# Down-projection by seven products: another order, and three of four weight sums by accumulating DMA

## The chip, the cores and the metric

The kernel runs on one core of one Trainium2 chip. The metric is the device time in microseconds of one execution; lower is better. Engines are named as in the profile: PE is TensorE's matmul, PEld its weight load, DVE is VectorE, ACT is ScalarE, POOL is GpSimd, SP is the queue that issues most DMAs.

## The reference, cut to what matters

One layer of a hybrid decoder on 256 positions of 2048 channels, all in float32. The change touches only the last product of the feed-forward part:

```
h = rmsnorm(x, g_ffn)                                   # 256 x 2048
u = causal_dwconv(h @ w_up, ffn_conv_w) + ffn_conv_b    # 256 x 11264
gate, val = split(u, 2)                                 # 256 x 5632 each
x = x + (silu(gate) * val) @ w_down                     # w_down: 5632 x 2048
out = rmsnorm(x, g_final)
```

## The kernel before

A float32 product is made of three matmuls: each operand is split into a coarse part `hi` and a rest `lo`, and hi x hi, hi x lo and lo x hi are added up in PSUM. A weight tile is therefore loaded as raw float32 by a DMA, ScalarE copies it to `hi` (rounding), VectorE subtracts `hi` from the raw tile into `lo`, and TensorE streams both. There are three buffers each for `raw`, `hi` and `lo`, so a split can be at most three tiles ahead of TensorE.

The feed-forward part works in six groups of hidden channels: five of 1024 and one of 512. `up` computes the hidden channels of a group from 8 tiles of `w_up` per 512 channels (24 matmuls a tile). The down-projection of a group follows one group later, and its products are put between the up tiles by hand: `sched` takes three up tiles, then an up tile and a product in turn, and after the last up tile of the group two products in a row. In the last, smaller group the products are packed more tightly.

The down-projection of a group of 1024 hidden channels and 1024 output channels (`p` is 0 or 1, so two of these per group) is one "block": a 2 x 2 block product done with seven products instead of eight. The stationary operands are the sums of activation blocks that `make_forms` makes once per group (`turn`, `sums`). The moving operands are weight blocks and sums of them, each 128 x 2048 float32 (1 MiB): products 0 to 6 use b11, b11+b12, b11+b12+b22, b12+b22, b22, b21 and b11+b12+b22+b21. These are held in three buffers of the tile `ffn` (`rawd`; a fourth part of `ffn` is `u_raw`). A sum is made in place, once the product that needed the earlier state of the buffer has been split. Two ways are used: `add`, a VectorE tensor_tensor of two buffers (L247), and `add_far`, a DMA issued by GpSimd that reads the second operand from DRAM and adds it into the buffer (L244). Plain loads are issued by SP (L241).

In class `Blocks` the products are done in the order 0, 1, 2, 3, 4, 5, 6. After the split of product 0, b12 is added to b11 by VectorE and b22 to b12 by DMA; after that of product 1, b22 is added to b11 by VectorE; after that of product 3, b21 is loaded into b12's buffer and added to b11 by DMA. After the splits of products 4, 5 and 6 the next block's b11, b22 and b12 are loaded into the buffers that have come free. The same class serves the output projection (`OutBlocks`) and part of the first up-projection (`UpBlocks`). Nine blocks of the down-projection are of class `Blocks`; the tenth is `Plain`, four ordinary products. The instructions between the head and the last group are ordered per engine by the framework's scheduler, which works from the program's order and its own estimate of when operands are ready; the order is fixed when the kernel is built.

Of the kernel before, what the change touches and what calls it, by code (L numbers as in the profile page):

```python
# [9 lines left out]
F32 = mybir.dt.float32  # L10
F32R = mybir.dt.float32r
AF = mybir.ActivationFunctionType
ALU = mybir.AluOpType
AX = mybir.AxisListType

P = 128
# [8 lines left out]
def kernel(  # L25
# [6 lines left out]
    nc = tc.nc  # L32
# [9 lines left out]
    x, mem, out = x[0], mem[0], out[0]  # L42
# [4 lines left out]
    wpool = ctx.enter_context(tc.tile_pool(name="wpool", bufs=3))  # L47
# [37 lines left out]
    def columns_turn(st, n, at):  # L85
        pt = bank(f"pcol_{at}")
        with tc.high_priority():
            nc.tensor.transpose(pt[:, :n], st[:n, :], ident[:n, :n])
            nc.vector.tensor_copy(cols[:, at : at + n], pt[:, :n])
        return at + n  # L90
# [13 lines left out]
    loaded, split = {}, {}  # L104
# [100 lines left out]
    group_of = []  # L205
# [7 lines left out]
    N_PROD = 7  # L213

    class Blocks:
# [12 lines left out]
        def at(self, name):  # L228
            return (self.seq + {"b11": 0, "b22": 1, "b12": 2, "b21": 2}[name]) % 3

        def buf(self, name):
            return rawd[self.at(name)]
# [16 lines left out]
        def split(self, i, idx):  # L249
            raw = self.buf(("b11", "b11", "b11", "b12", "b22", "b21", "b11")[idx])  # L250
            hi, lo = split[i] = [
                wpool.tile([P, 4, 512], F32R, tag=t, name=f"{t}_{i}") for t in ("hi", "lo")
            ]
            nc.scalar.activation(hi, raw, AF.Copy)  # L254
            nc.vector.tensor_tensor(lo, raw, hi.bitcast(F32), op=ALU.subtract)  # L255
            if idx == 0:
                self.add("b11", "b12")
                self.add_far("b12", "b22")
            elif idx == 1:
                self.add("b11", "b22")  # L260
            elif idx == 3:
                self.load("b21")
                self.add_far("b11", "b21")
            elif self.next is not None and idx >= 4:
                names = Plain.ORDER if isinstance(self.next, Plain) else ("b11", "b22", "b12")
                self.next.load(names[idx - 4])

    class Plain(Blocks):

# [1 line left out]
        ORDER = ("b11", "b21", "b12", "b22")  # L271

        def buf(self, name):
            return rawd[(self.seq + self.ORDER.index(name)) % 3]

        def split(self, i, idx):
            raw = self.buf(self.ORDER[idx])
# [38 lines left out]
    for gi in range(len(group_of) - 1):  # L316
        for p in range(2):

            kind = Plain if gi == len(group_of) - 2 and p == 1 else Blocks
            blocks.append(kind(len(blocks), gi, p))  # L320
            if len(blocks) > 1:
                blocks[-2].next = blocks[-1]
# [32 lines left out]
    prods = []  # L355
    for gi, (a, n) in enumerate(group_of):
        n_t = 8 * n
        if not prods:
            after = [0] * n_t
        elif n == 2:  # L360
            after = [0, 0, 0] + [1] * 12 + [2]
        else:
            after = [0, 0, 0, 1, 1, 1, 2, 6]
        assert sum(after) == len(prods)
        for t in range(n_t):
            if gi == 0:
                if t == 0:
                    for o in UP_ORDER:
                        sched.append(("up", 0, o) if isinstance(o, int) else ("mixed", UpBlocks.U, o[1]))
                continue  # L370
            sched.append(("up", a + t // 8, t % 8))
            for _ in range(after[t]):
                sched.append(prods.pop(0))
        if gi < len(group_of) - 1:
            prods = []
            for b in blocks[2 * gi : 2 * gi + 2]:
                n = len(b.ORDER) if isinstance(b, Plain) else N_PROD
                prods += [("plain" if isinstance(b, Plain) else "prod", b, i) for i in range(n)]
    for what, a, b in sched:
        if what == "up":  # L380
            w, q = part_of(a, b)
# [7 lines left out]
    a0, n = group_of[-1]  # L389
# [145 lines left out]
    at = columns_turn(*stage_g)  # L535
# [13 lines left out]
    for k in range(KC):  # L549
        i, j = divmod(k, 4)  # L550
# [41 lines left out]
    at = columns_turn(*stage_x)  # L592
# [20 lines left out]
    for i in range(KC // 4):  # L613
        ti = KC // 4 + i
        advance(ti + 1 + LOAD_AHEAD, 0)
        hi, lo = split.pop(ti)
# [201 lines left out]
    for j in range(0, NCONV, 2):  # L818
# [4 lines left out]
        for mi in range(2):  # L823
            t = spool.tile([P, S], F32, tag="w1k", name=f"cc_{j + mi}", bufs=6)
# [9 lines left out]
        for mi in range(2):  # L834
# [4 lines left out]
            t = spool.tile([P, S], F32, tag="w1k", name=f"cv_{j + mi}", bufs=6)  # L839
# [12 lines left out]
        for mi in range(2):  # L852
            t = spool.tile([P, S], F32, tag="w1k", name=f"cb_{j + mi}", bufs=6)
# [108 lines left out]
    rawd = [ffn[:, 1 + i, :].rearrange("p (j c) -> p j c", c=512) for i in range(3)]  # L962
# [306 lines left out]
```

## Time and profile before

| | |
|---|---|
| runs, median of 3 | 1039.08 us (1039.08 to 1039.49) |
| profiled execution, its own time | 1039.66 us |
| profiled execution, span | 1037.9 us |
| granted TensorE clock | 0.997 |
| HBM read | 222.06 MB, 216 GB/s over the span |

The span is the time from the first to the last instruction that the profile shows; the execution's own time is a little longer. A stretch of a profile gives the busy time of each engine in microseconds, with the number of its instructions in brackets, then the granted clock, the mean busy share of the sixteen DMA engines and GB/s. A timeline row gives start, duration, engine, line, operation, the tiles written and read, and in square brackets the engine's idle time just before and what ended it. In the chain of work that ended last, a row gives start, duration, engine, tile, line and the number of instructions.

### The profile page before, as it was taken

The page shows a single profiled execution, that of the slowest core. Times are in us where ns is not written, and L with a number is a line of the kernel's source. Part 1 is how long each engine was busy: PE and PEld are TensorE (multiplying, and loading weights), DVE is VectorE, ACT ScalarE, POOL GpSimd, SP SyncE. Part 2 cuts the span into 40 slices and gives each one's busy share as a digit, 9 for nine tenths or more (in the row PEclk, how much of TensorE's full clock was granted, in tenths as well). Part 3 has the DMA queues.
Part 4 walks back from the last instruction along what each step waited for, and adds up shares of the span by engine and source line. Part 5 has one row for each costly group of instructions (what it writes and reads, how often), then busy time and mean ns, then how long its engine had stood idle before and what let it go on. Part 6 is the DMA issues. An engine that isn't in the chain of part 4 may idle for free.

```text
span 1037.9 us, 12624 instructions
## 1 busy us (share of the span) xinstructions
PE 1026.7 (99%) x4970; PEld 861.9 (83%) x4970; DVE 820.5 (79%) x866; ACT 601.8 (58%) x654; POOL 64.1 (6%) x97
## 2 busy tenths in 40 slices
PE   9999999999999999999999999999999999999996
PEld 7888888888888888888888888888888888888885
DVE  5677686777869688978779787797878978789776
ACT  5965454544556576655556556665566655665653
POOL 0023500000001000000000000000000000000000
PEclk9999999999999999999999999999999999999998
DMA  9765465557775687687966878668786697867832
GB/s 321 254 214 191 146 201 175 191 191 240 220 262 176 155 259 243 197 253 203 259 224 201 255 204 260 219 199 258 208 260 216 194 265 209 258 218 191 282 118 81
DMA packets 125157, 224.97 MB, mean 217 GB/s; under 512 B 3970, under 2 KB 36010, under 8 KB 124970
## 3 DMA queue, kind: packets, MB, share of 16 engines
q1 hardware_dynamic: 113450, 201.09, 57.2%
q0 software_dynamic: 11616, 23.07, 13.6%
q8 instruction: 39, 0.64, 0.2%
q14 instruction: 20, 0.16, 0.1%
q10 hardware_dynamic: 32, 0.01, 0.0%
HBM read 222.06 MB, written 2.10 MB: 216 GB/s over the span
## 4 chain that ended last, share of the span: by engine, by line
PE 98%; DMA 1%; DVE 0%; SPq 0%; DVEq 0%; issue 0%; ACT 0%
PE pu L981 42%; PE pp_a L921 9%; PE pp_b L921 5%; PE pp_c L921 2%; PE pa_cb L468 2%; PE pa_pv L468 2%; PE pa_cx L468 2%; PE pa_cc L468 2%; PE po L504 2%; PE pp L1127 2%; PE po L501 2%; PE po L507 2%; PE pz L1079 2%; PE pm_a L1024 2%; PE pa_q L468 1%; PE pk L558 1%
## 5 line engine op out<-in xcount | busy, mean ns | idle before, releaser
L981 PE MATMUL pu<-hi,h2T 128*128 128x512 f32 x1280 | 409.4, 391 | 0.0
L132 DVE TENSOR_TENSOR lo<-raw,hi 128x2048 fp32r<-128x2048 f32 (+3 forms) x148 | 314.7, 2128 | 70.9 <-ACT hi L131 69.9
L131 ACT ACTIVATE hi<-raw 128x2048 fp32r<-128x2048 f32 (+3 forms) x148 | 264.3, 1789 | 110.5 <-issue 34.7
L981 PEld LDWEIGHTS pu<-hi,h2T 128*128 128x128 f32 x1280 | 240.3, 188 | 49.4
L981 PE MATMUL pu<-lo,h2T 128*128 128x512 f32 x640 | 249.5, 390 | 0.0
L255 DVE TENSOR_TENSOR lo<-ffn,hi 128x2048 fp32r<-128x2048 f32 x70 | 160.3, 2290 | 72.0 <-ACT hi L254 72.0
L254 ACT ACTIVATE hi<-ffn 128x2048 fp32r<-128x2048 f32 x70 | 134.0, 1916 | 105.1 <-PE pu L981 75.0
L981 PEld LDWEIGHTS pu<-lo,h2T 128*128 128x128 f32 x640 | 120.2, 188 | 25.1 <-DVE lo L132 0.7
L921 PE MATMUL pp_a<-hi,sums 128*128 128x512 f32 x288 | 94.5, 389 | 0.0
L1089 DVE SCALAR_TENSOR_TENSOR t<-pz,cols,t 128x255 f32<-128x255 f32 (+1 forms) x176 | 79.6, 478 | 10.2 <-ACT t L1087 9.2
L1087 ACT ACTIVATE t<-pz,cols 128x256 f32<-128x256 f32 x88 | 46.9, 558 | 48.1 <-DVE t L1089 24.2
L921 PEld LDWEIGHTS pp_a<-hi,sums 128*128 128x128 f32 x288 | 54.1, 188 | 11.2
L244 POOL DMA_DIRECT2D ffn<-in_w_down_dram x18 | 23.1, 1284 | 575.8 <-DVE ffn L247 454.3
L921 PE MATMUL pp_a<-lo,sums 128*128 128x512 f32 x144 | 56.0, 389 | 0.0
L1005 ACT ACTIVATE z<-pu,r_x 128x512 f32<-128x512 f32 x40 | 27.4, 686 | 39.7 <-PE pu L981 39.6
L247 DVE TENSOR_TENSOR ffn<-ffn 128x2048 f32<-128x2048 f32 x20 | 45.7, 2287 | 3.4 <-DMA ffn<-in_w_up_dram 3.4
L921 PE MATMUL pp_b<-hi,sums 128*128 128x512 f32 x144 | 47.3, 389 | 0.0
L921 PEld LDWEIGHTS pp_a<-lo,sums 128*128 128x128 f32 x144 | 27.0, 188 | 5.6
L921 PEld LDWEIGHTS pp_b<-hi,sums 128*128 128x128 f32 x144 | 27.0, 188 | 5.6
L468 PE MATMUL pa_cb<-hT,hi 128*128 128x512 f32 x96 | 30.7, 400 | 0.0
L468 PE MATMUL pa_pv<-hT,hi 128*128 128x512 f32 x96 | 30.2, 396 | 0.0
L468 PE MATMUL pa_cc<-hT,hi 128*128 128x512 f32 x96 | 30.2, 395 | 0.0
(292 smaller groups left out, 1477.1 us busy)
## 6 DMA issues: line engine op xcount, KB each, us to landing
raw<-in_w_up_dram SPq DMA_DIRECT2D x84, 1024.0 KB, 7.5
ffn<-in_w_down_dram SPq DMA_DIRECT2D x40, 1024.0 KB, 6.1
raw<-in_w_in_dram SPq DMA_DIRECT2D x28, 1024.0 KB, 5.0
ffn<-in_w_down_dram POOLq DMA_DIRECT2D x18, 1024.0 KB, 10.3
raw<-in_w_out_dram SPq DMA_DIRECT2D x12, 1024.0 KB, 5.1
raw<-in_w_kv_dram SPq DMA_DIRECT2D x4, 1024.0 KB, 7.3
outp<-in_w_out_dram SPq DMA_DIRECT2D x4, 1024.0 KB, 7.5
ffn<-in_w_up_dram SPq DMA_DIRECT2D x4, 1024.0 KB, 5.5
```

Of the source, the lines that this page charges most:

```text
L131: nc.scalar.activation(hi[:, s, :], raw[:, s, :], AF.Copy)
L132: nc.vector.tensor_tensor(lo[:, s, :], raw[:, s, :], hi[:, s, :].bitcast(F32), op=ALU.subtract)
L244: nc.gpsimd.dma_start(self.buf(to), self.source(what), accum_op=ALU.add)
L247: nc.vector.tensor_tensor(self.buf(to), self.buf(to), self.buf(what), op=ALU.add)
L254: nc.scalar.activation(hi, raw, AF.Copy)
L255: nc.vector.tensor_tensor(lo, raw, hi.bitcast(F32), op=ALU.subtract)
L468: nc.tensor.matmul(ps[mi], hi[:, kk, c], actT[:, k, :], start=first and kk == 0, stop=False)
L921: nc.tensor.matmul(ps, a, b[:, j, :], start=first and j == 0 and n == 0, stop=j == 3 and n == 2, skip_group_check=True,)
L981: nc.tensor.matmul(ps[tb], x_, y_[:, kk, :], start=k == 0 and n == 0, stop=k == KC - 1 and n == 2,)
L1005: nc.scalar.activation(z[tb], ps[tb], AF.Copy, scale=r_2[0][:, tb : tb + 1])
L1087: nc.scalar.activation(t, v, AF.Identity, bias=cvec("ffn_conv_b", m), scale=cw[2])
L1089: nc.vector.scalar_tensor_tensor(t[:, s:], v[:, : S - s], cw[2 - s], t[:, s:], op0=ALU.mult, op1=ALU.add)
```

## The change

The down-projection's blocks get a class of their own, `DownBlocks`. Its products are done in the order 0, 5, 1, 4, 2, 3, 6. Three sums of a block are accumulating DMAs (b11 += b12, b12 += b22, b11 += b21) and one is done by VectorE (b11 += b22). b12 is loaded inside the block, after the split of product 5, into the buffer that held b21; the previous block loads b11, b21 and b22. The assignment of the three buffers is changed to fit, in `Plain` too. Each accumulate reads its operand from DRAM, so a block reads 7 MiB instead of 6. `OutBlocks` and `UpBlocks` stay as they were, apart from the names that `UpBlocks` loads for the first block.

```
+    class DownBlocks(Blocks):
+        IDX = (0, 5, 1, 4, 2, 3, 6)
+        FIRST = ("b11", "b22", "b21")
+
+        def at(self, name):
+            x = self.seq % 2
+            return {"b11": x, "b22": 1 - x, "b21": 2, "b12": 2}[name]
+
+        def split(self, i, idx):
+            raw = self.buf(("b11", "b11", "b11", "b12", "b22", "b21", "b11")[idx])
...
+            after = self.next
+            names = after.ORDER if isinstance(after, Plain) else ("b11", "b21", "b22")
+            if idx == 0:
+                self.add_far("b11", "b12")
+            elif idx == 5:
+                self.load("b12")
+                self.add_far("b12", "b22")
+            elif idx == 1:
+                self.add("b11", "b22")
+            elif idx == 2:
+                self.add_far("b11", "b21")
+            elif after is not None and idx in (4, 3, 6):
+                after.load(names[(4, 3, 6).index(idx)])
...
     class Plain(Blocks):
         def buf(self, name):
-            return rawd[(self.seq + self.ORDER.index(name)) % 3]
+            return rawd[(1, 2, 0, 1)[self.ORDER.index(name)]]
...
-            kind = Plain if gi == len(group_of) - 2 and p == 1 else Blocks
+            kind = Plain if gi == len(group_of) - 2 and p == 1 else DownBlocks
...
+                    prods += [("prod", b, i) for i in b.IDX]
```

More of the change, by code (lines that the diff above doesn't have):

```diff
@@ L264, in split @@
             elif self.next is not None and idx >= 4:
-                names = Plain.ORDER if isinstance(self.next, Plain) else ("b11", "b22", "b12")
-                self.next.load(names[idx - 4])
+                self.next.load(self.next.FIRST[idx - 4])
+    class DownBlocks(Blocks):
[6 more added lines that the diff above has]
+            raw = self.buf(("b11", "b11", "b11", "b12", "b22", "b21", "b11")[idx])
+            hi, lo = split[i] = [
+                wpool.tile([P, 4, 512], F32R, tag=t, name=f"{t}_{i}") for t in ("hi", "lo")
+            ]
+            nc.scalar.activation(hi, raw, AF.Copy)
+            nc.vector.tensor_tensor(lo, raw, hi.bitcast(F32), op=ALU.subtract)
+            after = self.next
[11 more added lines that the diff above has]
+                after.load(names[(4, 3, 6).index(idx)])
     class Plain(Blocks):
@@ L376 @@
             for b in blocks[2 * gi : 2 * gi + 2]:
-                n = len(b.ORDER) if isinstance(b, Plain) else N_PROD
-                prods += [("plain" if isinstance(b, Plain) else "prod", b, i) for i in range(n)]
+                if isinstance(b, Plain):
+                    prods += [("plain", b, i) for i in range(len(b.ORDER))]
+                else:
+                    prods += [("prod", b, i) for i in b.IDX]
     for what, a, b in sched:
```

## The prediction

> **What bounds the kernel now.** I read the page's busy shares first, then the chain, then one period of the down-projection as a stretch, then each engine's timeline at the spots where the change puts something new.
>
> ```profile
> PE 1026.7 (99%) x4970; PEld 861.9 (83%) x4970; DVE 820.5 (79%) x866; ACT 601.8 (58%) x654; POOL 64.1 (6%) x97
> L247 DVE TENSOR_TENSOR ffn<-ffn 128x2048 f32<-128x2048 f32 x20 | 45.7, 2287 | 3.4 <-DMA ffn<-in_w_up_dram 3.4
> q0 software_dynamic: 11616, 23.07, 13.6%
> ffn<-in_w_down_dram SPq DMA_DIRECT2D x40, 1024.0 KB, 6.1
> ffn<-in_w_down_dram POOLq DMA_DIRECT2D x18, 1024.0 KB, 10.3
> 665.43:794.52 129.09, 129.07 (x586) 106.92 (x585) 107.02 (x97) 76.03 (x67) 5.16 (x4) 1.00 0.77 228
> ```
>
> The last row is one group: 16 up tiles and the 14 products of two blocks in 129.09 us, of which TensorE is busy 129.07. VectorE works 107.02 of it, ScalarE 76.03, and the DMA engines are busy 0.77 of it. The chain of TensorE pieces says the same with finer grain:
>
> ```profile
> 687.24 0.23 PE pu L981
> 691.18 2.73 PE pu L981 x12
> ...
> 780.03 5.44 PE pu L981 x24
> ...
> 788.19 2.72 PE pp_a L921 x12
> 790.91 2.73 PE pu L981 x12
> 794.52 5.68 PE pu L981 x25
> ```
>
> Twelve matmuls take 2.72 us wherever they stand, 0.23 each, and pieces follow without a gap. The one visible loss is where a group's new activations are formed: half an up tile with its eight transposes takes 691.18 - 687.24 = 3.94 us there and 794.52 - 790.91 = 3.61 elsewhere. That is 0.33 us, at most 1.3 over the four such places. So nothing can be gained beyond 1.3 us, and what the change does to the time is decided by whether it makes TensorE wait.
>
> **The change, part by part.** Nine DownBlocks run; a tenth block is Plain. The matmuls, the 63 splits and the additions into xt are the same in number, so TensorE's own work costs 0.
>
> *VectorE sums.* Two of 2.287 us per block become one: 9 x 2.287 = 20.6 us off VectorE. It ends on TensorE only if VectorE is late for TensorE, so at the 0.33 us places. There the next split of an up tile waits on ScalarE, behind the formation of the sums:
>
> ```profile
> 681.02 1.92 ACT L896 ACTIVATE sums<-turn 128x2048 fp32r<-128x2048 f32 x1 [4.33 <-DVE turn L895]
> ```
>
> The VectorE subtraction behind that ACTIVATE needs its result at 682.94, and the removed sum stood in just that wait. Bounds: 0 to 1.3 us gained. I take 0.
>
> *More DMA.* Per block four loads stay four loads, and two accumulates become three. The software queue took 13.6% of 1037.9 us for 23.07 MB, 6.1 us per MB, so 9 x 1.05 MB add 58 us of all sixteen engines, over some 560 us: the share of 0.77 goes to about 0.87. A raw load has room: this one is split by ScalarE 14.7 us after it is issued.
>
> ```profile
> 776.26 0.37 SPq L120 DMA_DIRECT2D raw<-in_w_up_dram  x1
> 790.95 1.92 ACT L131 ACTIVATE hi<-raw 128x2048 fp32r<-128x2048 f32 x1 [0.80 <-DVE xt L927]
> ```
>
> Even a transfer as slow as an accumulate lands within that, so I take 0. Without that cover ScalarE would wait, and each microsecond of it would reach TensorE.
>
> *The new waits.* A sum done by VectorE could be read at once. One done by DMA starts when the VectorE half of the previous split has ended, and the ScalarE half of the next product that reads the buffer waits for its landing. What is queued behind that wait on ScalarE is every later split and eviction. Here is what one accumulate takes, at two places in the second block of a pair (the first of these queries is 757 to 758 us, the second 498.9 to 499.2), what all 22 of the kernel take (third row), and how soon GpSimd starts it:
>
> ```profile
> DMA to landing us min/median/max: 10.4/10.4/10.4
> DMA to landing us min/median/max: 10.1/10.1/10.1
> DMA to landing us min/median/max: 9.2/10.3/11.9
> 697.27 2.29 DVE L255 TENSOR_TENSOR lo<-ffn,hi 128x2048 fp32r<-128x2048 f32 x1
> 699.86 1.28 POOL L244 DMA_DIRECT2D ffn<-in_w_down_dram  x1 [15.09 <-DVE lo L255]
> ```
>
> 697.27 + 2.29 = 699.56, start 699.86: 0.30 us. I take 10.3 from start to landing, the median, which is also the middle of the two nearest rows.
>
> Three accumulates per block, against the times at which ScalarE now takes the splits of the same places:
>
> ```profile
> 737.65 2.29 DVE L255 TENSOR_TENSOR lo<-ffn,hi 128x2048 fp32r<-128x2048 f32 x1 [1.55 <-ACT hi L254]
> 745.81 2.29 DVE L255 TENSOR_TENSOR lo<-ffn,hi 128x2048 fp32r<-128x2048 f32 x1 [0.87 <-ACT hi L254]
> 752.55 1.91 ACT L254 ACTIVATE hi<-ffn 128x2048 fp32r<-128x2048 f32 x1
> 769.19 1.92 ACT L254 ACTIVATE hi<-ffn 128x2048 fp32r<-128x2048 f32 x1 [1.24 <-PE pu L981]
> 777.35 1.92 ACT L254 ACTIVATE hi<-ffn 128x2048 fp32r<-128x2048 f32 x1 [3.52 <-PE pu L981]
> 780.07 1.92 ACT L254 ACTIVATE hi<-ffn 128x2048 fp32r<-128x2048 f32 x1 [0.80 <-PE pp_b L921]
> 782.79 0.69 ACT L1005 ACTIVATE z<-pu,r_x 128x512 f32<-128x512 f32 x1 [0.80 <-PE pu L981]
> 785.51 0.69 ACT L1005 ACTIVATE z<-pu,r_x 128x512 f32<-128x512 f32 x1 [2.03 <-PE pu L981]
> 786.10 1.91 ACT L131 ACTIVATE hi<-raw 128x2048 fp32r<-128x2048 f32 x1
> ```
>
> First (b11 += b12, after the first product's split, wanted by the third): 737.65 + 2.29 + 0.30 + 10.3 = 750.5, asked at 752.55. Hidden, 2.0 us to spare; without that cover its price would be the lateness itself. Second (b12 loaded after the second product's split, then b12 += b22, wanted by the sixth): 745.81 + 2.29 = 748.1, + 6.1 for the load, + 0.3 + 10.3 = 764.8, asked at 777.35. Hidden, 12.5 to spare. SP waits to 748.1 for that load, with raw loads behind it that are themselves released by later splits; on GpSimd only the third accumulate stands behind it. Third (b11 += b21, after the fifth product's split, wanted by the seventh), first block of a pair: an up tile of 5.44 us stands between the sixth and the seventh product, so there is 5.4 us more room than in the second block below, where the wait comes to 4. Hidden.
>
> Third, second block of a pair: here the sixth and the seventh product follow each other without an up tile between, so the distance is shorter by one up tile. These are the VectorE rows of that spot, and one of the formation that follows (from the group before):
>
> ```profile
> 771.14 2.29 DVE L255 TENSOR_TENSOR lo<-ffn,hi 128x2048 fp32r<-128x2048 f32 x1 [1.50 <-ACT hi L254]
> 788.03 2.29 DVE L132 TENSOR_TENSOR lo<-raw,hi 128x2048 fp32r<-128x2048 f32 x1 [3.65 <-ACT hi L131]
> 797.47 1.72 DVE L1089 SCALAR_TENSOR_TENSOR t<-pz,cols,t 128x255 f32<-128x255 f32 x4 [0.17 <-ACT t L1087]
> 675.68 2.29 DVE L255 TENSOR_TENSOR lo<-ffn,hi 128x2048 fp32r<-128x2048 f32 x1 [0.38 <-ACT hi L254]
> ```
>
> 771.14 + 2.29 + 0.30 + 10.3 = 784.03, but ScalarE asks at 780.07: it stands still 4 us. Then hi to 785.98, lo from 786.01 to 788.30. TensorE wants lo with its second matmul, at 788.19 + 0.23 = 788.42. So the product itself is just in time. But the two evictions (0.59 apart) follow, so the next up tile's hi starts about 787.1 instead of 786.10, its lo at 789.05 instead of 788.03 and ends 791.34; TensorE wants it at 790.91 + 0.23 = 791.14, so 0.25 us late with the handover. VectorE is now 1.0 us behind on its way into the formation of the sums, with idle time of 0.17 and 0.38 to take up: 0.45 late, 0.2 more than TensorE already is. Together 0.45 us, in each of four groups: 1.8. At 10.1 it would be about 0.25 each, at 10.4 0.55. Both ends: 0 each if the transfer lands by 9.8, 2 each if it takes 11.9, the slowest of the 22.
>
> *The last group* (one DownBlock, then Plain) has the fourth to seventh products packed tighter.
>
> ```profile
> 961.96 2.29 DVE L255 TENSOR_TENSOR lo<-ffn,hi 128x2048 fp32r<-128x2048 f32 x1 [1.06 <-ACT hi L254]
> 965.55 2.28 DVE L255 TENSOR_TENSOR lo<-ffn,hi 128x2048 fp32r<-128x2048 f32 x1
> 972.48 3.72 ACT L254 ACTIVATE hi<-ffn 128x2048 fp32r<-128x2048 f32 x2 [2.40 <-DMA ffn<-in_w_down_dram]
> 981.73 2.72 PE pp_a L921 x12
> ```
>
> Fifth split ends 967.83, landing 967.83 + 0.3 + 10.3 = 978.4, hi and lo to about 982.7, wanted at 981.96: 0.8 late. The one VectorE sum now comes after the third split, 2.29 us with 1.06 idle ahead of the fourth: the fifth split can slip by 0 to 1.2; I take 0.6. With 0.3 for the Plain split queued behind: 1.7.
>
> Sum: 1.8 + 1.7 + 0 - 0 = 3.5 us on the profiled execution's 1039.66, which lies 0.58 above the median of the runs: 1043.2 there, 1042.6 against the median of 1039.08.
>
> The Trainium skill, "DMA: Bandwidth & Descriptors", section "Anatomy of one DMA — SWDGE (gpsimd) path", fits such a transfer by about 2.0 us plus bytes over 436 GB/s, an estimate of 4.4 us for 1 MiB. The trace disagrees, with 10.1 to 10.4; by the page the sum above would be 0.
>
> **The rivals.** *Hidden after all.* The third accumulate costs nothing if it lands by about 9.8 us after its start, or if the scheduler puts the eviction of 782.79 ahead of the late hi. For it: the lateness is under half a microsecond each. Against a reordering: the scheduler seems to count a transfer shorter than it is.
>
> ```profile
> 335.70 0.37 SPq L241 DMA_DIRECT2D ffn<-in_w_up_dram  x1
> 338.82 1.92 ACT L131 ACTIVATE hi<-raw 128x2048 fp32r<-128x2048 f32 x1 [3.57 <-PE pu L981]
> 341.25 2.29 DVE L247 TENSOR_TENSOR ffn<-ffn 128x2048 f32<-128x2048 f32 x1 [3.38 <-DMA ffn<-in_w_up_dram]
> ```
>
> VectorE stood before this sum although a split's hi was ready at 340.74, so in its plan the load of 335.70 had landed within 5 us. If it treats an accumulate likewise, the order of the rows stays. Time: 1038 to 1040, taken as 1039.1, not slower; it decides from a landing of 9.8 us downwards. By the page's fit above this is the case that comes true.
>
> *Another order on ScalarE.* If the scheduler puts both evictions first, the seventh product's hi runs from 786.10 and its lo ends at 790.3, 1.9 late against 788.42 in four groups: 7.7 + 1.7, so 1048.5. It needs a scheduler that counts the accumulate at over 11 us; the same row speaks against that.
>
> *TensorE is not the bound.* Were VectorE what the stage waits for, 20.6 us would come off: 1018.5. Against it are the pieces of 2.72 us without gaps. The Trainium skill, "Perfetto Trace Analysis", section "Identifying the Most-Contended Engine", says that matmul busy time misleads and that weight-load busy time is to be read; that is 83% here, which would leave TensorE room. The constant spacing decides against it. This is also the case that the change does nothing of what relieving VectorE could bring.
>
> **How the numbers follow.** The chances: third accumulate late as worked out, 0.55; hidden, 0.36; other order, 0.06; VectorE the bound, 0.03. A measurement tells about 0.2%, 2.1 us, from no change. Of the first case 0.07 stays below that: landings of 10.1 and no slip in the last group give 4 x 0.25 + 1.1 = 2.1. So slower 0.48 + 0.06 = 0.54, same 0.07 + 0.36 = 0.43, faster 0.03. The first case's own range is 1041.2 (that sum) to 1046.7 (landings of 11.0 and the full slip, 4 x 1.15 + 3.0). The range adds the hidden case below, 1038.8, and a little over 11.0 above, 1047; the other order and the gain of 20.6 us are left out.
>
> **What would show it.** Right: on ScalarE the hi of the seventh product in every second block waits some 4 us for the DMA; TensorE's pieces behind the seventh product start up to half a microsecond late; the third and sixth products wait for nothing; DVE L247 counts 11 with 25 us. Wrong: accumulates that land well under 10 us, or over 11 in the fuller traffic; a different order of hi, evictions and up tiles; raw loads that ScalarE waits for.

## The result, and the profile after

The changed kernel takes 1054.45 us (median of 4 runs, 1052.33 to 1054.55) against 1039.09: 1.0141 times as long, 95% interval 1.0129 to 1.0154. The forecast was 1042.6, with 1047 as its upper end. The direction is right; the loss is more than four times the size.

Three lines of the changed kernel's page, then idle times by engine, line and releaser (total, times, longest): ScalarE's for the accumulates, and all of TensorE's in the feed-forward part:

```profile
span 1052.6 us, 12660 instructions
PE 1031.8 (98%) x4970; PEld 864.7 (82%) x4970; DVE 801.0 (76%) x857; ACT 599.2 (57%) x654; POOL 75.7 (7%) x106
PE 77%; DMA 9%; issue 8%; ACT 3%; DVE 2%; POOL 1%; DVEq 0%; ACTq 0%; POOLq 0%
```
```profile
ACT hi L282 <- DMA ffn<-in_w_down_dram: 27.7, 5, 7.7
```
```profile
PE pu L1013 <- ACT hi L131: 3.9, 4, 1.7
PE pp L1159 <- ACT hi L311: 3.7, 1, 3.7
PE pu L1013 <- DVE lo L132: 2.9, 4, 0.7
```

The wait that the prediction named on ScalarE is there, five times: once in each of the four groups of two up units and once in the last group. VectorE lost 19.5 us of work and the kernel did not gain by it. The chain, which had been TensorE almost throughout, now has 9% of DMA in it.

Where the time went is read from the first product of each group. These are the first and the last of the five groups with products, in the kernel before (L921) and after (L953):

```profile
426.52 0.39 PE L921 MATMUL pp_a<-hi,sums 128*128 128x512 f32 x1
942.56 0.39 PE L921 MATMUL pp_a<-hi,sums 128*128 128x512 f32 x1
```
```profile
426.06 0.39 PE L953 MATMUL pp_a<-hi,sums 128*128 128x512 f32 x1
950.45 0.39 PE L953 MATMUL pp_a<-hi,sums 128*128 128x512 f32 x1
```

| us | before | after | difference |
|---|---|---|---|
| start to the first product | 426.52 | 426.06 | -0.46 |
| the four groups | 516.04 | 524.39 | +8.35 |
| first product of the last group to the end of the span | 95.34 | 102.15 | +6.81 |
| span | 1037.9 | 1052.6 | +14.7 |

So the prediction's two places are the right ones, with 8.35 where it had 1.8 and 6.81 where it had 1.7.

The end of one of the four groups in the changed kernel, first the third accumulate as the chain has it, then the timeline:

```profile
776.96 10.16 DMA ffn<-in_w_down_dram
```
```profile
787.23 1.92 ACT L282 ACTIVATE hi<-ffn 128x2048 fp32r<-128x2048 f32 x1 [4.73 <-DMA ffn<-in_w_down_dram]
789.18 2.29 DVE L283 TENSOR_TENSOR lo<-ffn,hi 128x2048 fp32r<-128x2048 f32 x1 [3.76 <-ACT hi L282]
791.03 0.39 PE L953 MATMUL pp_a<-hi,sums 128*128 128x512 f32 x1
792.13 2.29 DVE L132 TENSOR_TENSOR lo<-raw,hi 128x2048 fp32r<-128x2048 f32 x1 [0.66 <-ACT hi L131]
792.15 0.50 PE L1013 MATMUL pu<-hi,h2T 128*128 128x512 f32 x1 [0.73 <-ACT hi L131]
794.34 0.68 DVE L959 TENSOR_TENSOR xt<-xt,pp_a 128x512 f32<-128x512 f32 x1
794.48 0.51 PE L1013 MATMUL pu<-lo,h2T 128*128 128x512 f32 x1 [0.73 <-DVE lo L132]
795.29 0.39 PE L953 MATMUL pp_a<-hi,sums 128*128 128x512 f32 x1
```

The landing makes ScalarE wait 4.73 us, and the seventh product's lo ends at 791.47. That is 0.2 us after the sixth product's last matmul on TensorE (791.03 plus 0.23), as forecast. But the seventh product starts at 795.29 and not at about 791.5. TensorE is not idle just before it: pieces of the next up tile stand ahead of it, and they wait twice, 0.73 us each, for their own hi and lo. These are late because they are split behind the late hi. The scheduler, which orders TensorE as well, had put them there when the kernel was built.

What the seventh product would wait for without these pieces is the read in L959. The two products that now end a group are products 3 and 6, and both accumulate into the PSUM bank `a`. Product 6 goes on adding to what product 3 left there, and product 3's state must first be added to xt by VectorE. That read stands on VectorE behind two lo subtractions, and these behind the late hi. In the order before, products 4 (bank `b`) and 5 (bank `c`) stood between products 3 and 6; this row is followed by the prediction's of 788.19:

```profile
785.47 2.72 PE pp_c L921 x12
```

The Trainium skill, "PSUM — Partial Sum Buffer", section "PSUM bank collisions raise a hardware error", has the rule behind that dependence: what TensorE writes and VectorE reads is to be kept apart by the bank. The rows above agree but do not show the wait: the next matmul into bank `a` starts 0.27 us after L959's span ends (794.34 + 0.68 to 795.29), but also right behind the matmul before it. Experiment 1 shows it.

The last group, in the same kernel: the accumulate as the chain has it, then from the timeline the split that waits for it and TensorE's first matmul behind, then the stretches that follow (PE, PEld, DVE, ACT, POOL, then the granted clock, the DMA share and GB/s):

```profile
975.81 12.60 DMA ffn<-in_w_down_dram
```
```profile
988.51 1.91 ACT L282 ACTIVATE hi<-ffn 128x2048 fp32r<-128x2048 f32 x1 [7.75 <-DMA ffn<-in_w_down_dram]
993.43 0.79 PE L1159 MATMUL pp<-hi,sums 128*128 128x512 f32 x1 [3.74 <-ACT hi L311]
```
```profile
992.00:994.00 2.00, 0.57 (x1) 0.42 (x2) 1.34 (x2) 2.00 (x2) 0.00 (x0) 0.60 0.07 10
994.00:996.00 2.00, 2.00 (x10) 1.98 (x9) 2.00 (x2) 1.68 (x2) 0.00 (x0) 0.50 0.86 179
996.00:998.00 2.00, 2.00 (x6) 1.52 (x6) 2.00 (x2) 0.00 (x0) 0.00 (x0) 0.50 1.00 330
998.00:1000.00 2.00, 2.00 (x8) 1.58 (x7) 1.37 (x3) 0.00 (x0) 0.00 (x0) 0.69 0.87 328
```

The third accumulate takes 12.6 us, TensorE stands for 3.74, and after that its clock is at half until about 999: twelve matmuls of a product take 3.56 us there where they take 2.72, eight transposes 1.71 where they take 0.87. With the clock's share of those stretches (0.57 x 0.4 + 2 x 0.5 + 2 x 0.5 + 2 x 0.31) that is 2.8 us. 3.7 + 2.8 make up nearly all of the 6.81.

### The profile page after: what moved, and what is told of

Read it like the earlier page. It is cut to its first block, busy times and chain, and to the rows that moved or that the text cites. A ratio compares the mean times of both kernels' runs of the same rounds, so it can differ in the third digit from the quotient of the medians.

```text
span 1052.6 us, 12660 instructions
## 1 busy us (share of the span) xinstructions
PE 1031.8 (98%) x4970; PEld 864.7 (82%) x4970; DVE 801.0 (76%) x857; ACT 599.2 (57%) x654; POOL 75.7 (7%) x106
## 4 chain that ended last, share of the span: by engine, by line
PE 77%; DMA 9%; issue 8%; ACT 3%; DVE 2%; POOL 1%; DVEq 0%; ACTq 0%; POOLq 0%
PE pu L1013 29%; DMA ffn<-in_w_down_dram 9%; PE pp_a L953 6%; PE pp L1159 2%; PE pa_cb L500 2%; PE pa_cx L500 2%; PE pa_pv L500 2%; PE pa_cc L500 2%; PE po L536 2%; PE po L533 2%; PE po L539 2%; PE pp_b L953 2%; PE pm_a L1056 2%; PE pk L590 1%; PE pa_q L500 1%
## 5 line engine op out<-in xcount | busy, mean ns | idle before, releaser
L283 DVE TENSOR_TENSOR lo<-ffn,hi 128x2048 fp32r<-128x2048 f32 x63 | 144.3, 2291 | 104.2 <-ACT hi L282 104.1
L282 ACT ACTIVATE hi<-ffn 128x2048 fp32r<-128x2048 f32 x63 | 120.6, 1914 | 113.6 <-PE pu L1013 72.6
L953 PE MATMUL pp_a<-hi,sums 128*128 128x512 f32 x288 | 95.3, 392 | 0.0
L1121 DVE SCALAR_TENSOR_TENSOR t<-pz,cols,t 128x255 f32<-128x255 f32 (+1 forms) x176 | 79.1, 477 | 10.3 <-ACT t L1119 9.3
L244 POOL DMA_DIRECT2D ffn<-in_w_down_dram x27 | 34.6, 1283 | 584.1 <-DVE lo L283 437.4
L953 PEld LDWEIGHTS pp_a<-hi,sums 128*128 128x128 f32 x288 | 54.6, 189 | 11.6
L953 PE MATMUL pp_a<-lo,sums 128*128 128x512 f32 x144 | 56.4, 391 | 0.0
L953 PE MATMUL pp_b<-hi,sums 128*128 128x512 f32 x144 | 47.3, 389 | 0.0
L1125 ACT ACTIVATE t<-t 128x256 f32<-128x256 f32 x44 | 17.3, 411 | 28.8 <-DVE t L1121 28.8
L953 PEld LDWEIGHTS pp_a<-lo,sums 128*128 128x128 f32 x144 | 27.3, 190 | 5.7
L953 PEld LDWEIGHTS pp_b<-hi,sums 128*128 128x128 f32 x144 | 27.0, 188 | 5.6
```

Of the source, the lines that this page charges most:

```text
L244: nc.gpsimd.dma_start(self.buf(to), self.source(what), accum_op=ALU.add)
L953: nc.tensor.matmul(ps, a, b[:, j, :], start=first and j == 0 and n == 0, stop=j == 3 and n == 2, skip_group_check=True,)
L1121: nc.vector.scalar_tensor_tensor(t[:, s:], v[:, : S - s], cw[2 - s], t[:, s:], op0=ALU.mult, op1=ALU.add)
```

## The experiments

The theories by name. A: the late landing alone. B: the bank that products 3 and 6 share. T: the additional traffic. O: the order as such. W, in the texts on record before the first runs: the late landing together with TensorE's fixed order, before the shared bank was suspected.

**1. TensorE in the program's order.** `sched`'s loop is run with TensorE's order fixed to the program's, so the seventh product follows the sixth directly.

```
+    own_order.enter_context(tc.manual_schedule(engines={mybir.EngineType.PE}))
     for what, a, b in sched:
```

> The changed kernel, with TensorE alone kept in program order in the feed-forward part, so that the seventh product comes before the next up tile (and before the Plain product in the last group). The transfers and ScalarE's wait stay. Theory W with the fixed order as the larger half of the loss: at each of four group ends the loss falls from 2.2 us to the 0.5 that the prediction worked out, and in the last group TensorE waits some 3.3 us for the seventh product and, being idle for a little less long, may keep its clock: 1044 to 1045 us if it does, 1047 if not. If the order on TensorE does not matter: 1054 us. Theory T: 1054 us.

1071.31 us (1068.33 to 1076.21), ratio 1.0315 (1.0285 to 1.0345): far from the 1044 to 1047 expected, and the run that names the cause. Idle times of TensorE, then the seventh product's own lo, VectorE's read, the seventh product at one group end, and two of the stretches behind it:

```profile
PE pp_a L953 <- DVE xt L959: 19.8, 5, 4.1
```
```profile
796.80 2.29 DVE L283 TENSOR_TENSOR lo<-ffn,hi 128x2048 fp32r<-128x2048 f32 x1 [3.65 <-ACT hi L282]
801.97 0.68 DVE L959 TENSOR_TENSOR xt<-xt,pp_a 128x512 f32<-128x512 f32 x1
```
```profile
802.79 0.76 PE L953 MATMUL pp_a<-hi,sums 128*128 128x512 f32 x1 [3.64 <-DVE xt L959]
```
```profile
803.00:805.00 2.00, 2.00 (x5) 1.58 (x6) 1.85 (x1) 0.00 (x0) 0.00 (x0) 0.50 0.99 298
805.00:807.00 2.00, 2.00 (x6) 1.54 (x5) 0.00 (x0) 0.00 (x0) 0.00 (x0) 0.50 0.95 322
```

The seventh product's lo is ready at 799.09, and it starts at 802.79: it waits for the read of its bank, not for its own split. VectorE does the next up tile's lo first (799.76 to 802.05) although it stood idle for 0.66 us before that, so it is the order on VectorE, and not its load, that keeps the read back. The scheduler's reordering in the changed kernel was no loss but a cover: without it each group end has some 4 us of idle time (3.64 to 4.13), here with half the clock behind it, and a group takes 134.7 us.

**2. The pair taken apart.** The doubled place in a group's list moves from the last up tile to the tenth; products 3 and 6 of the second block get an up tile between them.

```
-            after = [0, 0, 0] + [1] * 12 + [2]
+            after = [0, 0, 0] + [1] * 6 + [2] + [1] * 6
```

> The changed kernel, with one number of the hand-written order moved: the two products without an up tile between them are the seventh of a group's first block and the first of its second block, no longer the sixth and seventh of the second block. The last group is left as it is. Theory W (the third accumulate, b11 += b21, lands too late for the seventh product where only one up tile lies between the fifth and the seventh, and TensorE, whose fixed order puts the first matmuls of the next up tile ahead of that product, stands still): the four group ends lose nothing, 8.3 us come back, the last group's 6.8 stay: about 1046 us. Theory T (the 9.4 MB more of DMA traffic slow all loads): nothing changes, 1054 us. Theory O (the new order of the products as such costs): 1054 us.

1044.28 us (1043.58 to 1044.98), 1.005 (1.0035 to 1.0065).

```profile
426.04 0.39 PE L953 MATMUL pp_a<-hi,sums 128*128 128x512 f32 x1
941.34 0.39 PE L953 MATMUL pp_a<-hi,sums 128*128 128x512 f32 x1
```

The four groups take 515.30 us, 128.83 each: all of their loss is gone and 0.74 us more. Bytes, sums and order are the changed kernel's, so T and O fall for the groups. The edit does not separate A from B, though. It also starts the third accumulate of the second block one up tile earlier, so ScalarE no longer waits for it at the group ends. Instead the first block's is late in two groups, by 4.77 and 4.20 us, at no price (128.86 and 128.82 us there).

The last group keeps its 101.9 us.

**3. No third accumulate.** b11 += b21 is left out, so the seventh product takes b11 + b12 + b22. The landing can't be late; the pair on bank `a` stays.

```
-            elif idx == 2:
-                self.add_far("b11", "b21")
```

> The changed kernel without the third accumulate (b11 += b21 after the fifth product) and with nothing in its place; the seventh product then uses b11+b12+b22, so the output differs. Theory A (the stall is the late landing of that accumulate): ScalarE does not wait, and the time falls to 1038 to 1040 us. Theory B (the stall is that the sixth and the seventh product, 3 and 6, add into the same PSUM bank: the seventh must wait until VectorE has read the bank into xt after the sixth, and VectorE does that only behind the next up tile's subtraction): at each of four group ends and in the last group TensorE still waits 2 to 3 us for xt, so 1048 to 1053 us. Where both matter, between: 1041 to 1047.

1045.04 us (1044.25 to 1045.88), 1.0054 (1.0041 to 1.0068).

```profile
426.06 0.39 PE L951 MATMUL pp_a<-hi,sums 128*128 128x512 f32 x1
945.96 0.39 PE L951 MATMUL pp_a<-hi,sums 128*128 128x512 f32 x1
```

129.98 per group, 1.15 more than in experiment 2: the price of B by itself. Pieces of the next up tile still stand ahead of the seventh product, and TensorE waits 0.72 us among them in each group. The last group takes 1042.5 - 945.96 = 96.5 us, so there the landing is what costs most; 1.2 us over the kernel before stay.

**4. An own bank for product 6.** Product 6 accumulates into a bank of its own, and VectorE adds both banks to xt. The landing stays late.

```
+        own = isinstance(bl, DownBlocks) and i == 6
+        if own:
+            chain, first = "d", True
...
+        if own:
+            nc.vector.tensor_tensor(o, o, chains["a"], op=op)
         nc.vector.tensor_tensor(o, o, ps, op=op)
```

> The changed kernel, with product 6 of the down-projection's blocks in a PSUM bank of its own and two additions into xt behind it (the bank of products 0, 2 and 3, and its own), 0.68 us more on VectorE per block. The third accumulate stays as late as it is. Theory B: the seventh product no longer waits for VectorE's reading; what stays is the 0.5 us per group end of the prediction and some 2 us in the last group: 1040 to 1043 us. Theory A: the landing is as late as before, 1053 to 1055 us.

1054.48 us (1054.18 to 1056.71), 1.015 (1.0136 to 1.0164), no better than the change itself. By the time alone that would speak for A (1053 to 1055); the trace tells another story. The first period, from the first group's first product to the next group's, shows the edit alone:

```profile
426.01 0.39 PE L956 MATMUL pp_a<-hi,sums 128*128 128x512 f32 x1
555.03 0.39 PE L956 MATMUL pp_a<-hi,sums 128*128 128x512 f32 x1
```
```profile
525.15 1.92 ACT L282 ACTIVATE hi<-ffn 128x2048 fp32r<-128x2048 f32 x1 [4.48 <-DMA ffn<-in_w_down_dram]
```
```profile
526.88 2.72 PE pp_a L956 x12
529.60 2.75 PE pp_d L956 x12
532.34 2.90 PE pu L1018 x12
```

ScalarE waits 4.48 us, the seventh product follows the sixth without a gap, and only the up tile behind it loses 0.17 us. That period is 129.02, which is 0.2 over experiment 2: the price of A by itself in this period, where the prediction had 0.45. From the second period on (131.9 to 132.9 us) the edit costs something of its own: the second product of the next group starts 5.6 us after the first where it took 9.1, and TensorE waits for its split there. The scheduler had drawn it forward, in both kernels with the additional bank in every block (this and the next). At the third and fourth group ends, where ScalarE waits 5.13 and 5.85 us, the seventh product also waits 0.28 and 0.99 us for its own lo, so A is not worth 0.2 everywhere.

```profile
560.65 0.50 PE L956 MATMUL pp_c<-hi,sums 128*128 128x512 f32 x1 [0.58 <-ACT hi L282]
```

**5. Both.** Experiments 3 and 4 together (the seventh product again without b21).

> Both: own bank for product 6 and no third accumulate (the output differs as in the run without it). Nothing of A or B is left: 1038 to 1039 us, the kernel before less up to 1.3 us where VectorE's lighter load shows at the places where a group's activations are formed. If it stays above 1041, a third cause exists.

1047.16 us (1045.95 to 1048.11), 1.0074 (1.006 to 1.0088), not the 1038 to 1039 expected, by the same side effect. Its first period is 128.80, as clean as in experiment 2; the others are 130.6, with TensorE waiting 0.8 us at most in each of four places for the split of the product drawn forward, and 0.57 us in four more for a split of an up tile.

The first period, which has no product drawn forward, in the four kernels:

| us | landing in time | landing late |
|---|---|---|
| own bank | 128.80 (experiment 5) | 129.02 (experiment 4) |
| shared bank | 129.97 (experiment 3) | 130.79 (the change) |

With both gone nothing is left of the loss there (128.86 in experiment 2). In the later periods experiment 4 takes 1.3 to 2.2 us more than experiment 5: beside a product drawn forward the late landing costs more than 0.2.

**6. The third sum replaced.** In place of b11 += b21 a second b12 += b22 is issued, so traffic stays and the seventh product waits for nothing (products 3 and 6 take other sums than they should).

```
+                self.add_far("b12", "b22")
                 self.add_far("b12", "b22")
...
-                self.add_far("b11", "b21")
```

> The changed kernel without b11 += b21 after the fifth product; in its place a second accumulate of b22 into b12 right behind the first one, so that the number of accumulating transfers and their bytes are the same (the seventh product then uses b11+b12+b22, the sixth b12+2 b22: the output differs). Theory W: no split waits for a late landing, since the second accumulate ends some 20 us after the second product's split and is wanted after about 30: 1038 to 1040 us, the kernel before. Theory T: the bytes are the same, 1054 us. Theory O: 1054 us.

1059.78 us (1058.42 to 1060.36), 1.0197 (1.0182 to 1.0213). The design was at fault: of two accumulates in series the second lands up to 15.5 us after its own start, and the sixth product's split waits for it (ScalarE waits 10 times for an accumulate, 50.9 us in all).

It says nothing on A against B; experiments 3 and 4 took its place.

**7. The last group's places.** The fourth and fifth products move one up tile earlier, and the sixth too. An up tile now stands between products 3 and 6, so the edit takes A and B together.

```
-            after = [0, 0, 0, 1, 1, 1, 2, 6]
+            after = [0, 0, 0, 1, 1, 3, 1, 5]
```

> The changed kernel, with only the last group's order moved: the first two products after an up tile each, then three products after one up tile, one after the next, and the seventh with the four Plain ones after the last, so that two up tiles lie between the fifth and the seventh product. Theory W: the last group's 6.8 us come back (the stall of 3.7 us and the half clock behind it), the four group ends keep theirs: about 1047.5 us, and the granted clock is 1.00 through the last group. Theories T and O: 1054 us. If the load of b12 with the accumulate behind it is now too tight for the sixth product (some 18 us against 17.5 to 22), a new wait of a microsecond or two shows there: 1048 to 1050.

1050.29 us (1049.73 to 1052.8), 1.0113 (1.0096 to 1.0129). The last group goes from 102.15 to 1049.0 - 951.62 = 97.4 us. The four groups, which the edit leaves alone, take 525.57 us where the changed kernel took 524.39; where these 1.2 us come from is not shown.

**8. Experiment 2, and a bank of its own for product 6 in the last group only.**

> The kernel with the pair of products moved to between the two blocks (the run that gave 1044.3) and, in the last group alone, product 6 in its own PSUM bank. By B, most of the last group's 6.5 us go (its stall of 3.8 us and the half clock behind it), and some 2 us of the late landing stay: 1039 to 1041 us. By A they stay: 1044 us.

1043.19 us (1041.38 to 1044.1), 1.0036 (1.0023 to 1.005), above the 1039 to 1041 expected by B and below A's 1044. The last group takes 1040.7 - 940.94 = 99.8 us against 101.9 in experiment 2. ScalarE still waits 7.3 us for the third accumulate, but TensorE's longest wait is 1.8 us in place of 3.8. Behind it the granted clock is 0.50 and 0.69 in the stretches from 984 to 988. So the bank is worth 2.1 us in the last group, and the landing more.

**9. Experiments 2 and 7 together.**

> The seven-product order kept in every block; in each group of two up units the pair of products that ended the group (3 and 6) is taken apart by moving the doubled place from the last up tile to the tenth; in the last group the fourth product moves from the seventh up tile to the sixth, and the second one with it. Theory B (what the change costs is the pair 3 and 6 that share an accumulation bank and stand side by side, with the late landing behind it; the two places where that happens, the four group ends and the last group, add up): the group ends give 8.3 us back as the run of the first edit alone showed, the last group 4.5 us (its time from first product to end of span was 97.2 us with the second edit alone, 101.7 without), so 1044.3 - 4.5 = 1039.8, within 1039 to 1041. Theory T (more bytes by DMA are what costs the rest): nothing of the traffic changes, so at least 1043.

1042.24 us (1040.57 to 1042.58), 1.0028 (1.0016 to 1.0039), above the 1039 to 1041 that was expected. The groups are clean (128.8 each). The last group takes 99.0 us where experiment 7 alone had 97.4, with the same idle time of TensorE. First experiment 9's row and the stretch behind it, then the same of experiment 7:

```profile
963.31 0.73 PE L1013 MATMUL pu<-hi,h2T 128*128 128x512 f32 x2 [1.77 <-ACT hi L131]
```
```profile
964.00:966.00 2.00, 2.00 (x7) 1.57 (x6) 2.00 (x2) 0.00 (x0) 1.05 (x1) 0.53 1.08 311
966.00:968.00 2.00, 2.00 (x7) 1.52 (x7) 0.27 (x1) 0.00 (x0) 0.00 (x0) 0.62 1.04 306
```
```profile
973.72 0.73 PE L1013 MATMUL pu<-hi,h2T 128*128 128x512 f32 x2 [1.77 <-ACT hi L131]
```
```profile
974.00:976.00 2.00, 2.00 (x10) 1.62 (x10) 2.00 (x2) 0.00 (x0) 1.28 (x1) 1.00 1.05 298
976.00:978.00 2.00, 2.00 (x11) 1.65 (x10) 0.78 (x2) 0.10 (x1) 0.00 (x0) 1.00 1.05 314
```

Behind the same 1.77 us, 2 x 0.47 + 2 x 0.38 = 1.7 us are lost to the clock in one execution and none in the other. That accounts for the difference between 99.0 and 97.4.

**10. The kernel before with experiment 2's list.** The control for the 0.74 us that experiment 2 gained over the kernel before.

> The kernel before, with the same one edit to the list of places (the doubled place moves from the last up tile to the tenth); its order of products and its sums on VectorE stay. It is the control for the 0.28 us per group of two units by which the first edit on the changed kernel ran shorter than the kernel before (128.81 against 129.09 us). If the lighter VectorE gave that, this kernel keeps 129.09 and ends at 1039.1; if the places gave it, this one has 128.8 as well and ends near 1037.9. If here the doubled place in the middle brings a product of its own before its split is ready, above 1039.5.

1045.39 us (1044.92 to 1045.52), 1.0061 (1.0047 to 1.0074). The old order does not bear these places: 130.5 per group, with a wait of its own (TensorE stands four times, 5.6 us in all, for the split of a product on bank `b`). So it can't serve as the control; the next run does.

**11. The kernel before without its first VectorE sum** (the second product takes b11, the third b11 + b22, and the seventh lacks b12 too).

```
-                self.add("b11", "b12")
+                if self.w is not w_down:
+                    self.add("b11", "b12")
```

> The kernel before, its order and places untouched, with the sum b11 += b12 on VectorE left out of the nine blocks of the down projection (so the third product takes b11 where it should take b11 + b12, plus b22): 9 x 2.29 = 20.6 us off VectorE, nothing added to the DMA queues, no new wait. It weighs one term by itself: what the lighter VectorE is worth to TensorE. Theory V (that sum stands ahead of the next split where a group's activations are formed, and costs TensorE 0.28 to 0.33 us in each of four groups): first products 128.8 us apart instead of 129.1, and a time of 1037.9, within 1037.5 to 1038.3. Rival (the 0.28 us came with the new order's places and buffers, and the sum stands in a wait for ScalarE, as the prediction took it): 129.1 apart and 1039.1.

1039.18 us (1039.1 to 1040.86), 0.9998 (0.9989 to 1.0007). The rival holds: the four groups take 515.91 us, 516.04 before. The sum stood in a wait, which is now open, and the loss at the formation is still there:

```profile
684.24 2.29 DVE L900 TENSOR_TENSOR sums<-turn,sums 128x2048 fp32r<-128x2048 f32 x1 [1.98 <-ACT sums L897]
```
```profile
688.52 0.24 PE pu L982
688.75 0.22 PE pz L1080 x2
688.97 2.78 PE pu L982 x11
691.75 0.65 PE pz L1080 x6
```

Eight transposes and twelve matmuls take 3.89 us here, much as before (3.94), and 2.73 + 0.87 = 3.60 in experiment 12's kernel at the same place. So the lighter VectorE does not bring that 0.3 us by itself; it comes with the new order and places. Three of the four groups have it: they took 129.05 to 129.15 us before and 128.80 to 128.82 in experiment 2, and the first group 128.74 and 128.86. Which of the rearrangements does it stays open.

**12. The last block in the old order.** Experiment 2, and the last of the nine seven-product blocks in the order 0 to 6 with its sums as before; the other eight keep three accumulates.

```
+    class LastDown(Blocks):
+        IDX = range(7)
+        AHEAD = ("b11", "b12", "b22")
+        def at(self, name):
+            return {"b11": 0, "b22": 1, "b12": 2, "b21": 2}[name]
```

> The changed kernel with the doubled place moved to the tenth up tile, and the last seven-product block (one of nine) put back to the order 0 to 6 with its first two sums on VectorE, as before; the other eight keep the new order with three sums by DMA. Theory B: the last group then takes the 95.2 us that it took before, from a first product at 941.5 us, which is a span of 1036.7 and a time of 1037.9 (between 1037.2 and 1039). If the last group's loss came from what the eight blocks ahead leave behind (traffic, buffers) and not from the late third sum in that block, it keeps 97 to 102 us: 1040 to 1044.

1038.59 us (1038.3 to 1040.22, 11 runs) against 1039.16 of the kernel before: 0.9996 (0.9987 to 1.0005). The time lies within the bounds of the sum (1037.9, 1037.2 to 1039).

```profile
941.13 0.39 PE L965 MATMUL pp_a<-hi,sums 128*128 128x512 f32 x1
```
The last group is back at 1036.5 - 941.13 = 95.4 us and TensorE has no wait in its feed-forward part. Eight of nine blocks with all three accumulates, 8.4 MB more than before, cost nothing that can be measured: traffic (T) is refuted here as well. The version is the best of all that ran, but its interval does not tell it from the kernel before.

## Why the prediction was wrong, point by point

*What bounds the kernel; VectorE's relief; traffic.* Right. The DMA share of one group (687.77 to 818.66), forecast at 0.87, is 0.86. In the changed kernel ScalarE waits for no raw load in the groups. The 20.6 us off VectorE were worth 0 where the prediction took 0: experiment 11 takes the sum at the formation away and nothing moves. About 0.3 us at three of the formations was gained after all (0.74 us in experiment 2), with the new order, within the 1.3 us given as the upper bound.

*First and second accumulate, and the third in the first block of a pair.* Right; ScalarE's five waits are all for the third, four in the second block of a pair and one in the last group.

*Third accumulate, second block.* The timing is right almost to the tenth: 10.2 us to land (10.3), ScalarE waits 4.73 (4), the split's lo is 0.2 us from the sixth product's end. Experiment 4 prices this lateness at 0.2 us in the first group (0.45). The step that failed is "So the product itself is just in time". It asked only when the seventh product's split would be ready, and not what its PSUM bank waits for, and it kept TensorE's order although the scheduler orders that anew. Products 3 and 6 side by side on one bank cost 1.15 us per group with a punctual landing (experiment 3). With the late one, the read of the bank stands behind the late splits on VectorE, the pieces put ahead of it wait for late splits too, and the two together cost 2.0 to 2.1 us in three of the groups and 3.0 in the fourth (130.79 to 131.79 against 128.83), where the landing was later still:

```profile
919.03 1.92 ACT L282 ACTIVATE hi<-ffn 128x2048 fp32r<-128x2048 f32 x1 [5.67 <-DMA ffn<-in_w_down_dram]
```

The prediction's last part named pieces behind the seventh product that "start up to half a microsecond late" as the sign that it is right. The seventh product itself started 4 us late (795.29 for 791.26), with pieces of the up tile ahead of it; that is the "different order" that the same part named as a sign of being wrong, on TensorE. Landings over 11 us, another of its signs, came at the fourth group end (11.1) and in the last group.

*The last group.* The term was mis-sized, 6.81 for 1.7. The accumulate took 12.6 us and not 10.3, the split that waits for it had two evictions and Plain's hi behind it, and the prediction had no term for a stall long enough to slow TensorE's clock: 2.8 us of the 6.8. The shared bank has a part here too: an own bank takes 2.1 us off (experiment 8), leaving out the third accumulate 5.6 (experiment 3). Experiment 12 shows that all of it hangs on this one block's order.

*The rivals.* None of the three came true. What was missing is a fourth: a dependence between two products that the new order makes neighbours. It could be read from the code before any run: the table of chains in `prod` gives bank `a` to products 0, 2, 3 and 6, and the new order ends in 3, 6.

## What to carry to other kernels

When operations are reordered, ask for each new pair of neighbours what they share on the output side (an accumulation bank, an eviction between them), not only when their inputs are ready. The lateness of one operand is not the price of a wait: here it cost nothing in experiment 2 and 3 us in the fourth group of the change. Price it with everything that stands behind it in the same engine's fixed order, and with the slower clock that followed every idle time of 3.6 us and more here, and some of 1.8. And when a change loses at the seams of an otherwise free rearrangement, put the seams back before giving up the whole: here one block out of nine and one entry of a list took back all 15 us.

## What the runs showed of the hardware

An idle time of 1.77 us on TensorE can be followed by half its clock or leave it alone: experiments 9 and 7 have the same row with either outcome. In experiment 7 an idle time of 2.10 us, at the fourth group end, leaves the clock at 1.00 too, so its length alone does not decide.

How long the clock stays at half follows from the granted clock of the stretches. In experiment 9 it is (2 x 0.47 + 2 x 0.38) / 0.5 = 3.4 us. After the 3.74 us of the change it is (2 x 0.40 + 2 x 0.50 + 2 x 0.50 + 2 x 0.31) / 0.5 = 6.8 us, and after the 3.64 us of experiment 1, with 0.59 and 0.70 in the stretches on either side of the two shown, 6.8 us as well. The idle times of 3.94, 4.13 and 4.04 us at the other three group ends of experiment 1 are followed by 3.4 us each.

The Trainium skill, "TensorE: Matmul & The Clock Gate", section "Part 1: The HAM clock gate (the "warmup" mystery)", puts the fall to half clock after an idle window of about 3.4 us and says that the window runs freely. The long idles agree, and 3.4 and 6.8 us at half clock are about one and two such windows. The 1.77 us of experiment 9 do not agree with 3.4 us as a threshold; that one outcome differs from the other would fit a window that does not start with the idle time, which no run here tests.

An accumulating DMA of 1 MiB took 8.9 to 12.6 us in the changed kernel, and up to 15.5 us as the second of two in series (experiment 6).
